# A two-layer encoder with 16 experts: two experts' rows kept on chip, a down product by column halves, the next layer's weights prepared at another place, a norm without GpSimd

## The chip, the cores and the metric

The kernel runs on one core of one Trainium2 chip. TensorE multiplies matrices, VectorE, ScalarE and GpSimd do the element work, and the DMA engines move data; each engine works through its own queue in order and waits at semaphores for the others. SyncE's queue (SP) starts most transfers. The metric is device time in microseconds: the median of several executions. Profiles are of one execution, and times within it count from the start of its span.

## What is computed

Two layers of: a mixer (three kinds of attention behind one input projection), a layer norm, a mixture of 16 experts of which each of 512 tokens takes two, and a layer norm. What matters here is the second half:

```python
h = layer_norm(DEEPNORM_ALPHA * h + mix, ln1_g[l], ln1_b[l])
ffn = grouped_moe(h, router_w, router_bias, exp_w_gate[l], exp_w_up[l], exp_w_down[l])
h = layer_norm(DEEPNORM_ALPHA * h + ffn, ln2_g[l], ln2_b[l])

def grouped_moe(h, ...):                  # h: 512 x 1024, all float32
    ...                                   # gates: two experts per token
    y = jnp.zeros_like(h)
    for e in range(N_EXPERTS):            # 1024 -> 512 -> 1024
        a = jax.nn.silu(h @ w_gate[e]) * (h @ w_up[e])
        y = y + dense_gates[:, e:e + 1] * (a @ w_down[e])
    return y
```

## The kernel before

**Numbers and weights.** A float32 product is made of three matmuls of rounded parts (`mm3`, L399 to L401): high times high, low times high, high times low. So every weight passes through two steps: a high part (`prep_hi`, on ScalarE, L368) and a low part (`prep_lo`, on VectorE, L375, or on GpSimd, L377). Weights stream in as pieces of 512 KB in one fixed list over both layers: `pump` (L323) issues the next load on SP as soon as a buffer is free and the limit `dma_limit` and the cap allow, and `prep` splits pieces up to `look` ahead of the one in use. One piece of each expert product is taken whole in float32 (L1640, L1665) and is not split. Pieces are named "g", "u", "d" for an expert's gate, up and down weights (four of each) and "c0", "c1", ... for the input projection of the next layer.

**An expert.** In `moe`, expert e has a tile of 128 gathered tokens. Its rows come by an indirect load from hD (`start`, L1559), are transposed on TensorE (`trans_x`, L1629) and evacuated in three pieces on ScalarE and VectorE (L1598 to L1600); then come the gate projection, the up projection, the product silu(g) * u (L1735, L1744), its transposes (`trans_a`, L1654) and the down product (`down`, L1665 and `mm3`). The result is scaled by the gate and added to yD in memory by an indirect scatter on GpSimd (L1564). yD starts as a copy of the normed rows, which `w_out` writes beside hD (L1353). The gate projection of expert e+1 is written between the up and the down product of expert e.

**The last expert.** Expert 15 (`LAST`) is not scattered: its scaled rows stay on chip as a high part (L1674, ScalarE) and a low part (L1675, VectorE). After scatter 14, GpSimd loads yD back into h (L1732). `add_rows` multiplies the kept rows by a one-hot matrix for each of four token tiles and two column halves (L1875) and adds them to h with a running sum (L1877, VectorE); the one-hots are transposed beforehand in `last_rows` (L1862, L1863).

**The last norm.** `ln` takes the sum, centres the tile (L719 on ScalarE and L720 on GpSimd for the first three tiles of layer 1, else L722 on VectorE), squares it on ScalarE (L707), raises the variance to the power -0.5 on GpSimd (L709) and makes the final pass on VectorE (L725). In layer 0 the next layer's transposes follow (`make_hT`, L736, evacuated by L738 and L739); in layer 1 each tile goes out by one DMA (L1891).

**What sets the order.** A list scheduler orders the instructions of each engine when the kernel is built, from the order in which the code is written and estimated durations; on the chip each engine keeps that order. `busy(n)` writes n dummy matmuls (L554).

Of the kernel before, what the change touches and what calls it, by code (L numbers as in the profile page):

```python
# [23 lines left out]
S = 512  # L24
# [25 lines left out]
LAST = 15  # L50
# [7 lines left out]
WARM3 = 0  # L58
PRL = (0,)
# [13 lines left out]
LNP = ((), (0, 1, 2))  # L73
# [11 lines left out]
CAPE = 5  # L85
# [174 lines left out]
class Kern:  # L260
# [65 lines left out]
    def prep(self):  # L326
        while self.i_prep < self.i_dma and self.i_prep < self.cur + self.look:
            p = self.pieces[self.i_prep]
            must = self.i_prep == self.cur
            if p.whole:  # L330
                self.i_prep += 1
                p.bufs, p.parts = (p.raw,), ()
                self.prep_low(self.i_prep - 1)
                continue
            if not must and self.used[1] + 2 > self.rcap:
                return
            hi = self.take(self.R)
            lo = self.take(self.R) if hi else None
            if lo is None:
                assert not must, (self.R.free, self.used)  # L340
                if hi:
                    self.give(hi)
                return
            p.bufs = (hi, lo)
            raw, p.hi, p.lo = p.raw.f[:, 0:p.n], hi.r[:, 0:p.n2], lo.r[:, 0:p.n2]
            p.parts = p.split(raw, p.hi, p.lo) if p.split else [(raw, p.hi, p.lo)]
            for (r, hi, lo) in p.parts:
                self.prep_hi(r, hi)
            self.i_prep += 1
            self.prep_low(self.i_prep - 1)  # L350
# [52 lines left out]
    def build_stream(self):  # L403
# [83 lines left out]
        for l in range(DEPTH):  # L487
            for j in range(4):
                P[idx[l, "u%d" % (NE - 1), j]].low = P[idx[l, "d%d" % (NE - 1), j]].low = "v"
                if l:  # L490
                    P[idx[l, "c0", j]].low = "g"
        self.pieces = P
        self.i_dma = self.i_prep = self.i_low = self.n_hi = self.n_lo = 0
        self.dma_limit = len(P)
# [217 lines left out]
    def ln(self, z, sums=None, pool=False, eps=LN_EPS):  # L712
        nc, v = self.nc, self.nc.vector
        self.iw += 1
        w = self.lnbuf[3 + self.iw % 2].f

        def centre(st):
            if pool:
                nc.scalar.activation(w, z, AF.Identity, bias=st[:, 1:2])  # L719
                nc.gpsimd.tensor_tensor(w, w, self.lnrow[0], OP.mult)  # L720
            else:
                v.scalar_tensor_tensor(w, z, st[:, 1:2], self.lnrow[0], op0=OP.add, op1=OP.mult)  # L722

        st = self.ln_stats(z, sums, centre, eps)
        v.scalar_tensor_tensor(z, w, st[:, 4:5], self.lnrow[1], op0=OP.mult, op1=OP.add)  # L725
# [25 lines left out]
    def token_major(self, l, c, evac, pre=None):  # L751
# [5 lines left out]
        for t in range(NT):  # L757
            if pre:
                self.make_hT(t)
                if l == 0 and t == 0:  # L760
                    self.busy(WARM2)
                if l in PRL:
                    if 0 < t < NT - 1:
                        pre(t + 1)
                elif t + 2 < NT:
                    pre(t + 2)
# [527 lines left out]
    def w_out_phase(self, l):  # L1294
# [11 lines left out]
        st, pl = [None] * NT, [None] * NT  # L1306

# [35 lines left out]
        def finish(t, fast):  # L1343
# [8 lines left out]
            for d in (self.hD, self.yD):  # L1352
                nc.sync.dma_start(d[128 * t:128 * (t + 1)], z)  # L1353
# [213 lines left out]
    def moe(self, l):  # L1567
# [88 lines left out]

        def down(e):
            pd = [self.psS.tile([128, 512], F32, name="S") for _ in range(2)]
            for k in range(4):
                i = self.idx[l, "d%d" % e, k]  # L1660
                P = self.get(i)
                for n in range(2):
                    ns = slice(512 * n, 512 * (n + 1))
                    if P.whole:
                        nc.tensor.matmul(pd[n], aW()[:, k], P.raw.f[:, ns], start=k == 0, stop=k == 3)  # L1665
                    else:
                        self.mm3(pd[n], aT(0)[:, k], aT(1)[:, k], P.hi[:, ns], P.lo[:, ns], k == 0, k == 3)
                self.done(i)
            if e >= LAST:
                self.ylast[e] = [self.unit(self.R) for _ in range(2)]  # L1670
                g = gt[e]
                for n in range(2):
                    hi, lo = [x.r[:, 512 * n:512 * n + 512] for x in self.ylast[e]]
                    nc.scalar.activation(hi, pd[n], AF.Copy, scale=g)  # L1674
                    v.scalar_tensor_tensor(lo, pd[n], g, hi.bitcast(F32), op0=OP.mult, op1=OP.subtract)  # L1675
                return
# [4 lines left out]

        i_x = trans_x(0)
        pg[0] = self.psA.tile([128, 512], F32, name="A")
        proj(0, "g", pg[0], 0, 2)
        with self.tc.issue_after(i_x.ins):
            start(1)
        proj(0, "g", pg[0], 2, 4)
# [6 lines left out]
        self.dma_limit = self.idx[l, "d%d" % (NE - 1), 3] + 1  # L1694
        for e in range(NE):
# [34 lines left out]
            if e == NE - 1:  # L1730
# [5 lines left out]
            if e + 1 < NE:  # L1736
                trans_x(e + 1)
            if e + GD < NE:
                start(e + GD)
            if e == NE - 2:  # L1740
                for i in gb:
                    bufs[i].free()
            proj(e, "u", pu[e], 0, 4,
                 lambda: v.tensor_mul(sa[:, 512:1024], sa[:, 0:512], pu[e]))  # L1744
            if e + 1 < NE:
                pg[e + 1] = self.psA.tile([128, 512], F32, name="A")
                proj(e + 1, "g", pg[e + 1], 0, 2, lambda: trans_a(e))
            else:
                trans_a(e)
            if e + GD + 1 < NE:  # L1750
# [3 lines left out]
            down(e)  # L1754
# [126 lines left out]
    def combine(self, l, t):  # L1881
# [3 lines left out]
        self.ln(z, [sm[:, 0:1], sm[:, 1:2]], t in LNP[l], LN_EPS / ALPHA ** 2)  # L1885
# [4 lines left out]
        if l == DEPTH - 1:  # L1890
            self.nc.sync.dma_start(self.out[0, 128 * t:128 * (t + 1)], z)  # L1891
# [150 lines left out]
```

## Time and profile before

| | |
|---|---|
| time, median of 3 runs | 1404.48 us (1400.59 to 1405.84) |
| the profiled execution | 1408.89 us |
| its span | 1406.8 us |
| TensorE busy | 1298.7 us, 92% of the span |
| VectorE busy | 1010.6 us, 72% |
| ScalarE busy | 802.4 us, 57% |
| GpSimd busy | 285.9 us, 20% |
| moved by DMA | 291.10 MB, mean 207 GB/s |

The profiled execution took 2.1 us more than its span. Busy matmul time is modelled, so a busy TensorE is not one at its peak; the granted clock tells at which of its two levels (1.2 or 2.4 GHz) a stretch ran, as a share of the full one. Layer 0's experts lie between about 355 and 682 us, layer 1's between about 1026 and 1378 us.

### The profile page before, as it was taken

What the parts mean: (1) busy time and instruction counts of PE and PEld (TensorE: products, weight loads), DVE (VectorE), ACT (ScalarE), POOL (GpSimd) and SP (SyncE); (2) the same over time, 40 slices, a digit from 0 to 9 for tenths busy, and PEclk for the clock granted to TensorE, in tenths of its full rate; (3) what the DMA queues carried; (4) which work ended last, traced back from release to release, by engine and by line L of the source; (5) the groups of instructions that cost most, each with busy time, mean ns of one, the idle gap of its engine ahead of it and who ended that gap; (6) DMA issues with size and microseconds to landing.
All of it is one profiled execution on the core that took longest, in us unless ns stands there. A gap on an engine that the chain in (4) does not pass through costs nothing. (4 is left out here: it accounts for less than half of the span.)

```text
span 1406.8 us, 18646 instructions
## 1 busy us (share of the span) xinstructions
PE 1298.7 (92%) x5986; PEld 959.7 (68%) x5994; DVE 1010.6 (72%) x2268; ACT 802.4 (57%) x1428; POOL 285.9 (20%) x217
## 2 busy tenths in 40 slices
PE   7999999989999999899699999998989999969993
PEld 5786766668677776676478666676867777656761
DVE  5768977766778777777445798868668877757765
ACT  5467855651566665566336776556146666545662
POOL 1012213332111111111300222234212111102113
PEclk8999999999999999999799999999999999989997
DMA  8411313356699998999610133315759999879983
GB/s 259 125 31 31 109 61 91 113 186 240 200 310 319 321 351 268 341 384 314 222 42 16 36 93 102 120 52 189 270 168 301 312 319 366 248 252 320 382 298 120
DMA packets 114138, 291.10 MB, mean 207 GB/s; under 512 B 19719, under 2 KB 42503, under 8 KB 114033
## 3 DMA queue, kind: packets, MB, share of 16 engines
q1 hardware_dynamic: 97824, 255.35, 51.7%
q0 software_dynamic: 11424, 32.43, 9.6%
q10 hardware_dynamic: 4784, 2.05, 0.6%
q8 instruction: 50, 0.82, 0.2%
q14 instruction: 56, 0.45, 0.1%
HBM read 268.13 MB, written 28.05 MB: 211 GB/s over the span
## 5 line engine op out<-in xcount | busy, mean ns | idle before, releaser
L368 ACT ACTIVATE slot<-arena 128x1024 fp32r<-128x1024 f32 (+3 forms) x145 | 125.7, 885 | 118.8 <-PE A L401 28.0
L368 ACT ACTIVATE slot<-slot 128x1024 fp32r<-128x1024 f32 x105 | 110.8, 1059 | 88.3 <-PE A L401 41.1
L375 DVE TENSOR_TENSOR slot<-slot,slot 128x1024 fp32r<-128x1024 f32 x99 | 121.0, 1224 | 54.7 <-ACT slot L368 51.4
L401 PE MATMUL S<-slot,rounded 128*128 128x512 f32 x368 | 151.2, 411 | 0.0
L401 PE MATMUL A<-slot,rounded 128*128 128x512 f32 x364 | 144.7, 398 | 0.0
L399 PE MATMUL S<-slot,rounded 128*128 128x512 f32 x312 | 137.5, 442 | 7.1 <-ACT rounded L738 4.6
L375 DVE TENSOR_TENSOR slot<-arena,slot 128x1024 fp32r<-128x1024 f32 (+2 forms) x95 | 105.6, 1113 | 43.8 <-ACT slot L368 41.7
L1564 POOL DMA_INDIRECT yD<-arena,ix x30 | 50.1, 1670 | 416.8 <-ACT rounded L1599 207.0
L400 PE MATMUL S<-slot,rounded 128*128 128x512 f32 x312 | 127.7, 409 | 3.3 <-DVE rounded L739 2.0
L399 PE MATMUL A<-slot,rounded 128*128 128x512 f32 x276 | 121.4, 440 | 0.6 <-ACT rounded L738 0.6
L377 POOL TENSOR_TENSOR slot<-arena,slot 128x1024 fp32r<-128x1024 f32 (+4 forms) x50 | 80.1, 1617 | 174.7 <-ACT slot L368 153.5
L400 PE MATMUL A<-slot,rounded 128*128 128x512 f32 x276 | 109.9, 398 | 0.8 <-DVE rounded L739 0.8
L1955 ACT ACTIVATE arena<-arena,ast 128x256 f32<-128x256 f32 (+3 forms) x160 | 88.9, 557 | 32.7 <-DVE ast L1944 23.5
L368 ACT ACTIVATE rounded<-slot 128x1024 fp32r<-128x1024 f32 x74 | 78.5, 1061 | 44.2 <-PE A L400 27.7
L399 PE MATMUL S<-rounded,slot 128*128 128x512 f32 (+1 forms) x224 | 90.5, 406 | 0.0
L400 PE MATMUL S<-rounded,slot 128*128 128x512 f32 (+1 forms) x224 | 90.0, 402 | 0.0
L401 PE MATMUL S<-rounded,slot 128*128 128x512 f32 (+1 forms) x224 | 89.3, 399 | 0.0
L401 PEld LDWEIGHTS S<-slot,rounded 128*128 128x128 f32 x368 | 72.0, 196 | 16.8 <-DVE slot L1809 0.8
L399 PE MATMUL A<-rounded 128*128 128x512 f32 x172 | 81.5, 474 | 0.1
L1986 ACT ACTIVATE slot<-T 128x128 fp32r<-128x128 f32 (+3 forms) x128 | 53.4, 431 | 48.2 <-PE T L1981 47.5
L401 PEld LDWEIGHTS A<-slot,rounded 128*128 128x128 f32 x364 | 68.7, 189 | 15.9
L1640 PE MATMUL A<-slot,arena 128*128 128x512 f32 x168 | 79.3, 593 | 0.0
(365 smaller groups left out, 3062.1 us busy)
## 6 DMA issues: line engine op xcount, KB each, us to landing
slot<-in_exp_w_down_dram SPq DMA_DIRECT2D x80, 512.0 KB, 7.2
slot<-in_exp_w_up_dram SPq DMA_DIRECT2D x73, 512.0 KB, 6.9
slot<-in_exp_w_gate_dram SPq DMA_DIRECT2D x72, 512.0 KB, 6.9
arena<-in_exp_w_gate_dram SPq DMA_DIRECT2D x60, 512.0 KB, 6.5
arena<-in_exp_w_up_dram SPq DMA_DIRECT2D x59, 512.0 KB, 7.1
arena<-in_exp_w_down_dram SPq DMA_DIRECT2D x52, 512.0 KB, 6.9
arena<-in_w_in_dram SPq DMA_DIRECT2D x17, 512.0 KB, 5.5
slot<-in_w_in_dram SPq DMA_DIRECT2D x9, 512.0 KB, 6.1
```

Of the source, the lines that this page charges most:

```text
L368: self.nc.scalar.activation(hi, r, AF.Copy)
L375: self.nc.vector.tensor_sub(lo, r, hi.bitcast(F32))
L377: self.nc.gpsimd.tensor_tensor(lo, r, hi.bitcast(F32), OP.subtract)
L399: t.matmul(ps, xh, wh, start=start, stop=False)
L400: t.matmul(ps, xl, wh, start=False, stop=False)
L401: t.matmul(ps, xh, wl, start=False, stop=stop)
L1564: self.nc.gpsimd.indirect_dma_start(out=self.yD[:, :], out_offset=bass.IndirectOffsetOnAxis(ap=ix[:, 0:1], axis=0), in_=y, in_offset=None, ...
L1640: nc.tensor.matmul(ps, xW(e)[:, kk], P.raw.f[:, 512 * k:512 * k + 512], start=kk == 0, stop=kk == 7)
L1955: nc.scalar.activation(p, p, AF.Exp, bias=self.st[:, m:m + 1], scale=-1.0, accum_out=self.st[:, 2 + m:3 + m])
L1986: nc.scalar.activation(self.part(0), self.ps, AF.Copy)
```

## The change

- `LAST` is 14: the rows of experts 14 and 15 both stay on chip, and `add_rows` has four matmuls instead of two for each tile and half. The reload of h is written at expert 14, behind scatter 13. The last buffer of scattered rows is freed one expert earlier.
- `down_last`: expert 15's down product takes all four pieces for the left column half, keeps it, and then does the right half.
- The high and low parts of the next layer's pieces may be written right behind `trans_a(15)` (`prep_limit`), up to eight raw buffers may be used for them (`CAPE`), and the low parts of c0 are no longer on GpSimd. 18 dummy matmuls are written ahead of layer 1's first `make_hT`.
- The last norm does not use ScalarE and GpSimd for centring; its final pass and its output write are made by halves, the second half's write on ScalarE's queue.
- The writes of yD are issued behind all hD writes, in `moe` after the first gate matmuls. The transposes of expert 1 are written behind expert 0's up projection.

```diff
-LAST = 15
+LAST = 14
+WARM4 = 18
-LNP = ((), (0, 1, 2))
+LNP = ((), ())
-CAPE = 5
+CAPE = 8
...
-        while self.i_prep < self.i_dma and self.i_prep < self.cur + self.look:
+        while self.i_prep < min(self.i_dma, self.prep_limit, self.cur + self.look):
...
-                if l:
-                    P[idx[l, "c0", j]].low = "g"
...
-        v.scalar_tensor_tensor(z, w, st[:, 4:5], self.lnrow[1], op0=OP.mult, op1=OP.add)
+        if out is None:
+            v.scalar_tensor_tensor(z, w, st[:, 4:5], self.lnrow[1], op0=OP.mult, op1=OP.add)
+            return
+        for n in range(2):
+            ns = slice(512 * n, 512 * n + 512)
+            v.scalar_tensor_tensor(z[:, ns], w[:, ns], st[:, 4:5], self.lnrow[1][:, ns], op0=OP.mult, op1=OP.add)
+            (nc.scalar if n else nc.sync).dma_start(out[:, ns], z[:, ns])
...
+                if l and t == 0:
+                    self.busy(WARM4)
...
-            for d in (self.hD, self.yD):
-                nc.sync.dma_start(d[128 * t:128 * (t + 1)], z)
+            self.i_hd.append(nc.sync.dma_start(self.hD[128 * t:128 * (t + 1)], z))
...
+        def keep_rows(e, pd, n):
+            if n == 0:
+                self.ylast[e] = [self.unit(self.R) for _ in range(2)]
+            hi, lo = [x.r[:, 512 * n:512 * n + 512] for x in self.ylast[e]]
+            nc.scalar.activation(hi, pd, AF.Copy, scale=gt[e])
+            v.scalar_tensor_tensor(lo, pd, gt[e], hi.bitcast(F32), op0=OP.mult, op1=OP.subtract)
...
+        def down_last(e):
+            ids = [self.idx[l, "d%d" % e, k] for k in range(4)]
+            P = [self.get(i) for i in ids]
+            for n in range(2):
+                pd = self.psS.tile([128, 512], F32, name="S")
+                for k in range(4):
+                    down_mm(e, P[k], pd, k, n)
+                keep_rows(e, pd, n)
+            for i in ids:
+                self.done(i)
...
+        with ExitStack() as after:
+            for i in self.i_hd:
+                after.enter_context(self.tc.issue_after(i.ins))
+            for t in range(NT):
+                nc.sync.dma_start(self.yD[128 * t:128 * (t + 1)], self.h[:, t])
...
-            if e == NE - 1:
+            if e == LAST:
...
-            if e + 1 < NE:
+            if 0 < e < NE - 1:
...
+            if e == 0:
+                trans_x(1)
...
+                self.prep_limit = len(self.pieces)
+                self.budget(14, 2)
...
-            down(e)
+            (down if e + 1 < NE else down_last)(e)
...
-        self.ln(z, [sm[:, 0:1], sm[:, 1:2]], t in LNP[l], LN_EPS / ALPHA ** 2)
+        self.ln(z, [sm[:, 0:1], sm[:, 1:2]], t in LNP[l], LN_EPS / ALPHA ** 2,
+                None if l < DEPTH - 1 else self.out[0, 128 * t:128 * (t + 1)])
...
-        if l == DEPTH - 1:
-            self.nc.sync.dma_start(self.out[0, 128 * t:128 * (t + 1)], z)
```

Lines move by 1 (L399 becomes L400) to some 35 (L1875 becomes L1910). On TensorE at the MoE start of layer 0, before: the rows from the whole-precision part of expert 0's up projection (L1640) on.

```order
L1640 MATMUL A<-arena 128x512 x2
L1629 MATMUL T<-cst,arena 128x128 x8
L399 MATMUL A<-rounded 128x512
L400 MATMUL A<-rounded 128x512
L401 MATMUL A<-rounded 128x512
```

And now, the end of the same up projection and the start of expert 1's gate projection (L1647).

```order
L401 MATMUL A<-slot_3294,rounded 128x512
L402 MATMUL A<-slot_3295,rounded 128x512
L1636 MATMUL T<-cst,arena 128x128 x8
L1647 MATMUL A<-slot_2534,arena 128x512 x2
L400 MATMUL A<-rounded 128x512
```

The eight transposes of expert 1's rows stood ahead of the split part of expert 0's up projection and now stand behind its last matmul.

On ScalarE at the end of layer 0, before: three splits of expert 15's down weights, the evacuation of its activations (L1598, L1599), four splits of c0 between the two kept halves (L1674), and the squares of the norm.

```order
L368 ACTIVATE slot_6251<-arena 128x1024
L368 ACTIVATE slot_6261<-arena 128x1024
L368 ACTIVATE slot_6272<-arena 128x1024
L1598 ACTIVATE arena<-T 128x128
L1599 ACTIVATE rounded<-T 128x384
L368 ACTIVATE slot_6284<-arena 128x1024
L368 ACTIVATE slot_6310<-arena 128x1024
L368 ACTIVATE slot_6322<-arena 128x1024
L1674 ACTIVATE rounded<-S,gt 128x512
L368 ACTIVATE slot_6334<-arena 128x1024
L1674 ACTIVATE rounded<-S,gt 128x512
L707 ACTIVATE arena,bst<-h,bst 128x1024 x2
```

And now: the seven splits (slots 6333, 6321, 6315 and 6327 are c0's), the evacuation (L1605, L1606), both kept halves (L1669) and one split of c1.

```order
L369 ACTIVATE slot_6271<-arena 128x1024
L369 ACTIVATE slot_6333<-slot_6274 128x1024
L369 ACTIVATE slot_6282<-arena 128x1024
L369 ACTIVATE slot_6294<-arena 128x1024
L369 ACTIVATE slot_6321<-slot_6265 128x1024
L369 ACTIVATE slot_6315<-arena 128x1024
L369 ACTIVATE slot_6327<-slot_6267 128x1024
L1605 ACTIVATE arena<-T 128x128
L1606 ACTIVATE rounded<-T 128x384
L1669 ACTIVATE slot_6350<-S,gt 128x512 x2
L369 ACTIVATE slot_6369<-arena 128x1024
L706 ACTIVATE arena,bst<-h,bst 128x1024 x2
```

All four splits of c0 moved from behind the evacuation of expert 15's activations to ahead of it.

On GpSimd at the end of layer 1, before and then now:

```order
L569 DMA arena<-in_ln_b_dram 128x1024
L568 DMA arena<-in_ln_g_dram 128x1024
L1564 DMA yD<-arena,ix 640x1024
L1732 DMA h<-yD 128x1024 x4
L720 TENSOR_TENSOR arena<-arena 128x1024
L709 TENSOR_TENSOR bst<-bst,mhalf 128x1
L720 TENSOR_TENSOR arena<-arena 128x1024
```

```order
L1571 DMA yD<-arena,ix 640x1024
L1763 DMA h<-yD 128x1024 x4
L568 DMA arena<-in_ln_b_dram 128x1024
L567 DMA arena<-in_ln_g_dram 128x1024
L708 TENSOR_TENSOR bst<-bst,mhalf 128x1 x4
```

The scatter of expert 14 is gone, the reload of h moved ahead of the norm's rows and behind the scatter of expert 13, and the centring left this queue.

## Rows read from the trace of the kernel before

**Rows 1.** Stretches: us, busy time (instructions) by engine, granted clock, DMA share, GB/s.

```profile
1050.00:1190.00 140.00, 140.00 (x602) 101.17 (x601) 109.68 (x170) 89.59 (x118) 23.18 (x14) 1.00 0.96 320
...
675.00:680.00 5.00, 2.52 (x11) 1.69 (x9) 0.00 (x0) 2.00 (x2) 1.65 (x1) 1.00 1.04 409
```

**Rows 2.** TensorE's waits in the whole span: total us, times, longest.

```profile
PE S L1875 <- ACT rounded L1674: 7.5, 3, 5.1
PE T L1629 <- DMA arena<-hD,ix: 7.1, 2, 4.8
```

**Rows 3.** ScalarE's longest waits from 1050 to 1190.

```profile
ACT slot L368 <- PE A L401: 15.3, 18, 2.3
```

**Rows 4.** Timeline at both MoE starts: start, us, instruction, idle before and releaser.

```profile
362.22 1.58 PE L1629 MATMUL T<-cst,arena 128*128 128x128 f32 x8 [2.27 <-DMA arena<-hD,ix]
...
369.13 1.88 PE L1640 MATMUL A<-slot,arena 128*128 128x512 f32 x4
...
1028.94 1.96 PE L1640 MATMUL A<-arena 128*128 128x512 f32 x4
...
1035.74 1.94 PE L1629 MATMUL T<-cst,arena 128*128 128x128 f32 x8 [4.84 <-DMA arena<-hD,ix]
...
1042.38 1.88 PE L1640 MATMUL A<-arena 128*128 128x512 f32 x4
```

**Rows 5.** Timeline at layer 0's end; scatters' landing; low parts (page: busy, mean ns).

```profile
643.90 1.81 POOL L1564 DMA_INDIRECT yD<-arena,ix  x1 [14.52 <-ACT rounded L1599]
...
665.13 7.89 SPq L323 DMA_DIRECT2D arena<-in_w_in_dram  x4
...
669.66 3.55 PE L1665 MATMUL S<-slot,arena 128*128 128x512 f32 x4 [0.37 <-ACT arena L1598]
...
677.21 2.00 ACT L368 ACTIVATE slot<-arena 128x1024 fp32r<-128x1024 f32 x2 [7.22 <-DMA arena<-in_w_in_dram]
...
681.95 0.67 ACT L1674 ACTIVATE rounded<-S,gt 128x512 fp32r<-128x512 f32 x1
...
684.72 1.06 ACT L368 ACTIVATE slot<-arena 128x1024 fp32r<-128x1024 f32 x1 [2.10 <-DMA arena<-in_w_in_dram]
...
693.09 1.28 DVE L725 SCALAR_TENSOR_TENSOR h<-arena,bst 128x1024 f32<-128x1024 f32 x1
...
694.52 1.94 PE L736 MATMUL T<-cst,h 128*128 128x128 f32 x8 [3.71 <-DVE h L725]
...
DMA to landing us min/median/max: 6.2/9.1/12.5
...
L375 DVE TENSOR_TENSOR slot<-slot,slot 128x1024 fp32r<-128x1024 f32 x99 | 121.0, 1224 | 54.7 <-ACT slot L368 51.4
```

**Rows 6.** Timeline of layer 1's tail; landing of the output writes.

```profile
1379.71 0.69 DVE L1877 SCALAR_TENSOR_TENSOR h<-S,h 128x512 f32<-128x512 f32 x1
...
1381.65 0.15 DVE L702 TENSOR_TENSOR bst<-csum 128x1 f32<-128x1 f32 x1
...
1383.79 2.35 POOL L720 TENSOR_TENSOR arena<-arena 128x1024 f32<-128x1024 f32 x1 [9.79 <-ACT arena L719]
...
1384.35 1.81 DVE L702 TENSOR_TENSOR bst<-csum 128x1 f32<-128x1 f32 x1
...
1387.53 3.37 DVE L725 SCALAR_TENSOR_TENSOR h<-arena,bst 128x1024 f32<-128x1024 f32 x1 [0.56 <-POOL bst L709]
...
1393.00 3.25 DVE L722 SCALAR_TENSOR_TENSOR arena<-h,bst,arena 128x1024 f32<-128x1024 f32 x1
...
1398.99 1.28 DVE L725 SCALAR_TENSOR_TENSOR h<-arena,bst 128x1024 f32<-128x1024 f32 x1 [0.66 <-POOL bst L709]
...
DMA to landing us min/median/max: 2.6/2.6/2.6
```

**Rows 7.** All instructions of two lines: ns min/median/max, first and last start.

```profile
L1862 PE MATMUL T<-cst,arena x8: 271/272/273, 660.4 to 1363.1; 128*128 128x128 f32 x8
...
L554 PE MATMUL A<-mchunk,b_zero x46: 323/326/524, 1.4 to 13.5; 128*1 128x384 bf16 x46
```

More of the change, by code (lines that the diff above doesn't have):

```diff
@@ L489, in build_stream @@
                 P[idx[l, "u%d" % (NE - 1), j]].low = P[idx[l, "d%d" % (NE - 1), j]].low = "v"
[L490 to L491 removed]
         self.pieces = P
         self.i_dma = self.i_prep = self.i_low = self.n_hi = self.n_lo = 0
[L494 removed]
+        self.dma_limit = self.prep_limit = len(P)
         self.pat_hi, self.pat_lo = "a", "v"
@@ L710, in ln_stats, with ln @@
         return st
-    def ln(self, z, sums=None, pool=False, eps=LN_EPS):
+    def ln(self, z, sums=None, pool=False, eps=LN_EPS, out=None):
         nc, v = self.nc, self.nc.vector
@@ L1306, in w_out_phase @@
         st, pl = [None] * NT, [None] * NT
+        self.i_hd = []
         self.G = [self.psA.tile([128, 512], F32, name="A") for _ in range(2)]
@@ L1655, in trans_a, with down_mm @@
             parts(ps, aW(), aT(0), aT(1))
+        def keep_rows(e, pd, n):
[4 more added lines that the diff above has]
+            v.scalar_tensor_tensor(lo, pd, gt[e], hi.bitcast(F32), op0=OP.mult, op1=OP.subtract)
+        def down_mm(e, P, pd, k, n):
+            ns = slice(512 * n, 512 * (n + 1))
+            if P.whole:
+                nc.tensor.matmul(pd, aW()[:, k], P.raw.f[:, ns], start=k == 0, stop=k == 3)
+            else:
+                self.mm3(pd, aT(0)[:, k], aT(1)[:, k], P.hi[:, ns], P.lo[:, ns], k == 0, k == 3)
         def down(e):
@@ L1662, in down @@
                 for n in range(2):
[L1663 to L1667, printed above, removed]
+                    down_mm(e, P, pd[n], k, n)
                 self.done(i)
             if e >= LAST:
-                self.ylast[e] = [self.unit(self.R) for _ in range(2)]
-                g = gt[e]
                 for n in range(2):
-                    hi, lo = [x.r[:, 512 * n:512 * n + 512] for x in self.ylast[e]]
-                    nc.scalar.activation(hi, pd[n], AF.Copy, scale=g)
-                    v.scalar_tensor_tensor(lo, pd[n], g, hi.bitcast(F32), op0=OP.mult, op1=OP.subtract)
+                    keep_rows(e, pd[n], n)
                 return
@@ L1693, in moe @@
         self.ht, self.hts, self.ylast = {}, [], {}
-        self.dma_limit = self.idx[l, "d%d" % (NE - 1), 3] + 1
+        self.dma_limit = self.prep_limit = self.idx[l, "d%d" % (NE - 1), 3] + 1
         for e in range(NE):
```

## The prediction

> **What bounds the kernel now.** I read TensorE by stages first, then what it waited for, then what the engine that prepares its weights waited for, and last the order in time at the places where TensorE stood still. Inside the experts it has no hole: 140.00 of 140.00 us busy in a stretch of layer 1, with 602 matmuls, so 0.233 us each, at full clock [rows 1]. ScalarE's splits wait there for TensorE to give buffers back [rows 3], so weights come in time, although the DMA engines' share in the same stretch is 0.96 [rows 1]. An edit inside the experts can only add matmuls or not; what can be gained lies in the holes. TensorE's waits name the ones that this change touches [rows 2]: 7.1 us in two places for a gather (the MoE starts), and 7.5 us for the last expert's kept rows, nearly all at the end of layer 0. At that end it also waits 3.71 us for the norm [rows 5]. After the last matmul comes a tail of VectorE, ScalarE and GpSimd [rows 6].
>
> **MoE start (transposes of expert 1 behind expert 0's up projection).** TensorE stops before the eight transposes until the gather has landed, and 18 matmuls of the up projection, which need nothing of it, stand behind them [rows 4]. In layer 1 the whole-precision part of that projection starts at 1028.94 and takes 1.96 us, the transposes begin at 1035.74, and expert 1's gate projection at 1042.38. Turned round, the 18 matmuls run from 1030.9 for 18 x 0.233 = 4.2 us to 1035.1; the gather lands at 1035.7; the transposes take about 1.0 us instead of 1.94 if the clock stays up; their evacuation, with one split of 1.06 us ahead of it on ScalarE, takes some 1.1 us: the gate projection at 1037.8, a gain of 4.6 us. In layer 0 the stop of 2.27 us ended at 362.22 and the gate projection started at 369.13; the same working (gather at 362.2, matmuls to 364.2, transposes, evacuation) gives 366.4, a gain of 2.7. Against it, the yD writes are now issued behind all hD writes, the fourth close to the gather: 512 KB at the 320 GB/s of [rows 1] are 1.6 us, of which the gather feels 0 to 1.3, and in layer 1 that would show in full. Bounds: 2 to 3.5 and 3.5 to 5.8.
>
> **End of layer 0.** Three things followed each other [rows 5]. The next layer's first weights (four loads of 512 KB) were issued from 665.13 on, over 7.89 us. ScalarE's queue has their splits ahead of the last expert's kept rows, and it sat waiting for them: the first at 677.21 after 7.22 us of idle, the last at 684.72 after 2.10. The down product, four whole-precision matmuls in 3.55 us from 669.66 and 18 of 0.233, was done at about 677.4, but the first half of the kept rows came at 681.95. The norm's first tile was ready at 694.37 (693.09 + 1.28), and the transposes for the next projection began at 694.52. Now these loads and the reload of h stand behind the scatter of expert 13, issued at 643.90. Scatters took 6.2 to 12.5 us to land; with the median of 9.1 the first two pieces are issued near 654, the other two near 661, as buffers come free. All four splits now stand ahead of the evacuation of the last expert's activations on ScalarE, and one low part ahead of their product on VectorE, both queues in order: behind a split that waits are queued the evacuation, and behind that TensorE's whole down product. If the last piece takes 7 to 9 us it is there at 668 to 670, the evacuation is done at 671.3 and the down product starts at 671.8, 2.1 later than before. It runs at full clock, since dummies stand where TensorE idled: 18 x 0.233 and four whole ones in 1.9 (as the four at 1042.38 [rows 4]) are 6.1 us, to 677.9. The second half's kept rows take 0.67 on ScalarE (the length of the row at 681.95) and about as long on VectorE, to 679.4. VectorE then needs four sums of 0.69, one low part of 1.22, a centring and a final pass of 1.28 each, and 0.9 for small ones and the power: 7.4 us. The first tile is ready at 686.8 and the transposes start 7.6 us earlier; I take 7.2, since the norm's rows and other tiles share VectorE. Bounds: 2, if the last piece takes 12 us, as the first one did before (665.13 to 677.21), and the evacuation waits until 674; 10.5, if no split waits. The four low parts cost VectorE 4 x 1.22 = 4.9 us that GpSimd had; VectorE was busy 0.00 of the 5 us from 675 [rows 1], which is where they hide, and without that cover they would be 4.9 us of path.
>
> **Tail.** GpSimd's centring beside VectorE makes three VectorE instructions long [rows 6]: a 128x1 sum takes 1.81 us instead of 0.15 and ends when GpSimd's 2.35 us end; a final pass takes 3.37 instead of 1.28, a centring 3.25. That is 1.66 + 2.09 + 1.97 = 5.7 us, all on the chain, since VectorE idles there only in four waits for the power of 0.56 to 0.66. Without GpSimd they come back, and VectorE does three centrings more, 3 x 1.28 = 3.8. Eight final passes of half width (0.69, as a 128x512 sum) instead of four of 1.28 cost 0.4. Two of the four waits are now covered by work that stands behind them: 0.9 less. That is 2.4 us. The last output write is half as large, at 320 GB/s 0.8 us less at most; I take 0.4. Gain 2.8, bounds 1.5 to 4.5. The down product by halves gives nothing here: the second half is still evacuated behind the last matmul, and VectorE's first sum stands behind that.
> The four old output writes landed 2.6 us after issue, each alone [rows 6]. The Trainium skill (DMA: Bandwidth & Descriptors, Issuing engines are not separate DMA queues) says that transfers started by different engines end up on the same 16 DMA engines and interleave, which speaks against the second queue: by it the 0.4 would be due to the first half's earlier issue alone, and if both halves came at once the sum would be poorer by 0.4. No run here shows two output queues at once.
>
> **What the change adds.** Expert 14's one-hot transposes and their copies stand in the full expert stretch of both layers: four transposes of 0.27 [rows 7] and what they displace, 0.6 to 1.5 us a layer; I take 0.8, so 1.6. Of 16 more adding matmuls a layer, those of three tiles lie in holes; four stand inside the next projection, 4 x 0.233 = 0.9. One weight load is issued ahead of the overflow tile's, 0 to 1.6 us; I take 0.8. The 18 dummies lie in holes before the transposes, before the down product and between sums; at the low clock one costs 0.33 [rows 7], and those that don't fit add up to 3 us, which the lower bound of the transition holds. Scaling expert 14's rows twice instead of once takes ScalarE and VectorE 0.7 us each, off the path while TensorE is full; if that cover were gone it would be 0.7 a layer. The scatter that goes was on GpSimd, which nobody waits for inside the experts.
>
> **Sum.** -2.7 - 4.6 - 7.2 - 2.8 + 1.6 + 0.9 + 0.8 = -14.0 us. The profiled execution took 1408.89 us (its span of 1406.8 and 2.1 around it), 4.4 above the median of the runs; it would become 1394.9. Taken off the median, 1404.48 - 14.0 = 1390.5.
>
> **Rivals.**
> 1. The weights' stream is the bound. For it: a DMA share of 0.96 in the experts. What TensorE gains at the two MoE starts it then waits for later, in front of weights: -7.2 - 2.8 + 3.3 = -6.7, so 1397.8. Against it: ScalarE waited for TensorE, not for weights [rows 3]. Chance 0.14.
> 2. The next layer's pieces land 12 us after issue, as before; the transition gives 2 to 3: 1395.2. Chance 0.12.
> 3. Slower than before, by the same wait made longer. Each microsecond by which the last piece lands after 669 is one of the down product, since the evacuation stands behind its split. At 683, 22 us after issue, the whole gain is gone; at 25 us it is 1407.5, at 29 us 1411.5. For it: the last expert's weights, the reload of h and the norm's rows all want the DMA engines between 654 and 670. Against it: 12 us was what a piece took before, with the engines fully busy (share 1.04 from 675 on [rows 1]). Chance 0.04.
> 4. The change doesn't do what it says: the dummies don't hold the clock and run in TensorE's path, and the first tile of the norm comes no earlier. -2.7 - 4.6 - 2.8 + 3.3 = -6.8, and up to 3 for dummies: 1397.7 to 1400.7. Chance 0.06.
> 5. More than that: no split waits and every gain is at its upper bound, every cost at its lower: 3.5 + 5.8 + 10.5 + 4.5 - 2.2 = 22: 1382.4. Chance 0.06.
> The forecast, 1386 to 1395, has the rest, 0.58.
>
> **How the numbers follow.** About 0.5% (7 us) is what a measurement of this kernel can tell from no change; faster by more means under 1397.5. That holds the forecast 0.58, half of the first rival 0.07, the second 0.12 and the fifth 0.06: 0.83. Slower by more: 0.03 of the third and 0.02 for what I don't see, 0.05. The rest, 0.12, is the same. The range of 8 in 10 takes in the first two rivals and stops short of the fifth: 1383 to 1399.
>
> **What would show it.** TensorE's wait for the gather before expert 1's transposes should be under 1 us in both layers. From the last expert's first whole-precision down matmul to the first transposes of layer 1's input there should be some 15 us (before 669.66 to 694.52, 24.9). ScalarE should wait under 3 us for the next layer's pieces. No VectorE instruction of the tail should be longer than 1.4 us, and from its first sum to the end of the last pass there should be about 18.2 us (1379.71 to 1400.27, 20.6). A wait of TensorE inside the experts for weights that are not split, or one of ScalarE of 5 us or more ahead of the last evacuation, would make the sum wrong.

## The result, and the profile after

The changed kernel takes 1391.34 us (median; 1390.85 to 1393.26), the kernel before 1404.52 beside it: a ratio of 0.9894, 95% interval 0.9873 to 0.9916. In a second comparison on another chip the ratio was 0.9894 again (0.9861 to 0.9926), with runs of the changed kernel spread from 1385.6 to 1398.6. The forecast was 1390.5. The profiled execution took 1390.85 us, its span 1389.1; the one of before had been 4.4 us above its median, so the two profiles differ by 18.0 us and the medians by 13.2.

MoE starts, which answer to [rows 4]. Timeline of TensorE: start, duration, instruction, idle before and what ended it.

```profile
356.61 1.10 PE L1647 MATMUL A<-arena 128*128 128x512 f32 x2
...
363.65 1.05 PE L1636 MATMUL T<-cst,arena 128*128 128x128 f32 x8
...
365.23 1.98 PE L1647 MATMUL A<-slot,arena 128*128 128x512 f32 x4 [0.53 <-ACT arena L1605]
...
1021.06 1.10 PE L1647 MATMUL A<-arena 128*128 128x512 f32 x2
...
1027.81 1.13 PE L1636 MATMUL T<-cst,arena 128*128 128x128 f32 x8
...
1029.33 1.98 PE L1647 MATMUL A<-arena 128*128 128x512 f32 x4 [0.39 <-ACT arena L1605]
```

The transposes no longer wait for the gather, and they take 1.05 and 1.13 us (granted clock 1.00) instead of 1.58 and 1.94 (0.67 and 0.50). From the up projection's first whole matmul to expert 1's gate projection there are 8.62 and 8.27 us instead of 11.14 and 13.44. In layer 0 of the kernel before, that first matmul is this one:

```profile
357.99 1.96 PE L1640 MATMUL A<-arena 128*128 128x512 f32 x4
```

The end of layer 0, which answers to [rows 5]: timeline of the changed kernel.

```profile
649.99 7.73 SPq L324 DMA_DIRECT2D slot<-in_w_in_dram  x3
...
662.73 0.40 PE L402 MATMUL A<-slot,rounded 128*128 128x512 f32 x1
663.06 1.46 PE L553 MATMUL A<-mchunk,b_zero 128*1 128x384 bf16 x8
666.56 1.06 ACT L369 ACTIVATE slot<-slot 128x1024 fp32r<-128x1024 f32 x1 [6.53 <-DMA slot<-in_w_in_dram]
667.52 1.99 ACT L369 ACTIVATE slot<-arena 128x1024 fp32r<-128x1024 f32 x2
...
669.92 0.68 DVE L1775 TENSOR_TENSOR arena<-arena,A 128x512 f32<-128x512 f32 x1
...
670.66 1.13 PE L1661 MATMUL T<-cst,arena 128*128 128x128 f32 x4 [6.14 <-DVE arena L1775]
...
671.72 2.40 PE L553 MATMUL A<-mchunk,b_zero 128*1 128x384 bf16 x7
672.26 0.25 ACT L1605 ACTIVATE arena<-T 128x128 f32<-128x128 f32 x1
...
674.05 2.08 PE L1675 MATMUL S<-slot,arena 128*128 128x512 f32 x2
...
690.00 1.94 PE L741 MATMUL T<-cst,h 128*128 128x128 f32 x8 [2.42 <-DVE bst L703]
```

Here little was gained. The kept rows no longer wait, but TensorE stands for 6.14 us one step earlier, before the transposes of expert 15's activations: ScalarE waits 6.53 us for one of the next layer's pieces, and two splits of expert 15's own down weights stand behind it; VectorE's product L1775 stands behind the low parts of that piece and of the first of these, and the transposes wait for the product. On ScalarE three more splits of c0 stand ahead of the evacuation at 672.26, 5.7 us after the end of the wait. The last up matmul ends at 663.1, and layer 1's transposes start 26.9 us later; it was 27.6 before, where the last up matmul is this one:

```profile
666.54 0.40 PE L401 MATMUL A<-slot,rounded 128*128 128x512 f32 x1
```

(On ScalarE before, three of the four splits of c0 stood ahead of the first kept half and one between the halves; not all four stood between them.)

The tail, which answers to [rows 6]: VectorE in the changed kernel, the first sum, two passes of half width, the longest instructions, the last pass.

```profile
1365.13 0.68 DVE L1912 SCALAR_TENSOR_TENSOR h<-S,h 128x512 f32<-128x512 f32 x1
...
1369.33 0.15 DVE L701 TENSOR_TENSOR bst<-csum 128x1 f32<-128x1 f32 x1
...
1376.12 1.28 DVE L721 SCALAR_TENSOR_TENSOR arena<-h,bst,arena 128x1024 f32<-128x1024 f32 x1
...
1378.13 1.42 DVE L729 SCALAR_TENSOR_TENSOR h<-arena,bst 128x512 f32<-128x512 f32 x2 [0.41 <-POOL bst L708]
...
1381.47 1.42 DVE L729 SCALAR_TENSOR_TENSOR h<-arena,bst 128x512 f32<-128x512 f32 x2 [0.66 <-POOL bst L708]
```

No VectorE instruction is longer than 1.28 us (the 1.42 are two), and from the first sum to the last pass's end there are 17.8 us instead of 20.6.

**Stage by stage.** The next table is worked out from each kernel's timeline, in us between marks: MoE start (first gate matmul to expert 1's gate projection), experts (from there to the last up matmul's end), end of layer 0 (from there to layer 1's first transposes), input projection (from there to the transposes of L847, which follow it), mixer (to the first gate matmul), sums (last up matmul's end to the first sum), tail (to the end of the last pass), output (to the span's end).

| stage | before | before again | changed | changed again | splits behind (e2) | e11 |
|---|---|---|---|---|---|---|
| start of the span to layer 0's MoE | 351.7 | 353.6 | 350.3 | 352.4 | 348.0 | 351.8 |
| MoE start, layer 0 | 17.5 | 17.5 | 14.9 | 14.9 | 14.9 | 14.9 |
| experts, layer 0 | 297.8 | 298.3 | 297.9 | 300.7 | 299.7 | 300.2 |
| end of layer 0 | 27.6 | 27.9 | 26.9 | 21.6 | 18.2 | 17.4 |
| input projection | 38.5 | 38.3 | 36.2 | 37.0 | 35.6 | 35.6 |
| mixer, layer 1 | 289.6 | 289.5 | 288.6 | 289.6 | 289.4 | 289.2 |
| MoE start, layer 1 | 19.8 | 19.3 | 14.6 | 15.0 | 14.6 | 14.7 |
| experts, layer 1 | 326.9 | 325.7 | 325.5 | 329.4 | 325.9 | 327.5 |
| sums | 10.5 | 10.5 | 10.3 | 11.9 | 9.5 | 9.5 |
| tail | 20.6 | 20.5 | 17.8 | 17.8 | 17.8 | 17.8 |
| output | 6.5 | 6.5 | 6.2 | 6.2 | 6.2 | 6.2 |

What repeats within 0.5 us is the MoE starts, the tail and the output. The first 350 us, the mixer and the experts differ between executions of one kernel by as much as between kernels, so 1.4 + 1.0 + 1.4 = 3.8 us of the 17.7 by which the two spans differ lie in stretches where no run shows the edit to act.

### The profile page after: what moved, and what is told of

Read it like the earlier page. It is cut to its first block, busy times and chain, and to the rows that moved or that the text cites. A ratio compares the mean times of both kernels' runs of the same rounds, so it can differ in the third digit from the quotient of the medians.

```text
span 1389.1 us, 18769 instructions
## 1 busy us (share of the span) xinstructions
PE 1303.3 (94%) x6052; PEld 961.6 (69%) x6052; DVE 1016.0 (73%) x2289; ACT 800.3 (58%) x1429; POOL 267.3 (19%) x208
## 5 line engine op out<-in xcount | busy, mean ns | idle before, releaser
L376 DVE TENSOR_TENSOR slot<-slot,slot 128x1024 fp32r<-128x1024 f32 x105 | 128.3, 1225 | 64.7 <-ACT slot L369 61.9
L369 ACT ACTIVATE slot<-slot 128x1024 fp32r<-128x1024 f32 x111 | 117.1, 1058 | 100.4 <-PE A L402 36.7
L402 PE MATMUL A<-slot,rounded 128*128 128x512 f32 x372 | 147.7, 397 | 0.0
L400 PE MATMUL S<-slot,rounded 128*128 128x512 f32 x316 | 138.9, 442 | 6.4 <-ACT rounded L743 4.0
L376 DVE TENSOR_TENSOR slot<-arena,slot 128x1024 fp32r<-128x1024 f32 (+2 forms) x101 | 112.8, 1120 | 42.8 <-ACT slot L369 40.5
L400 PE MATMUL A<-slot,rounded 128*128 128x512 f32 x288 | 125.4, 435 | 0.3 <-ACT rounded L743 0.3
L1571 POOL DMA_INDIRECT yD<-arena,ix x28 | 46.9, 1674 | 408.1 <-ACT rounded L1606 197.5
L401 PE MATMUL A<-slot,rounded 128*128 128x512 f32 x288 | 114.1, 396 | 0.4 <-DVE rounded L744 0.4
L378 POOL TENSOR_TENSOR slot<-arena,slot 128x1024 fp32r<-128x1024 f32 (+4 forms) x46 | 70.7, 1550 | 170.2 <-ACT slot L369 148.6
L369 ACT ACTIVATE rounded<-slot 128x1024 fp32r<-128x1024 f32 x70 | 74.3, 1061 | 44.6 <-PE A L401 25.5
L400 PE MATMUL S<-rounded,slot 128*128 128x512 f32 (+1 forms) x224 | 90.5, 406 | 0.0
L402 PEld LDWEIGHTS S<-slot,rounded 128*128 128x128 f32 x368 | 70.9, 193 | 17.7 <-DVE slot L1844 2.0
L1647 PE MATMUL A<-slot,arena 128*128 128x512 f32 x168 | 79.4, 594 | 0.5 <-ACT arena L1605 0.5
L400 PEld LDWEIGHTS S<-slot,rounded 128*128 128x128 f32 x316 | 61.1, 194 | 25.4 <-ACT rounded L743 5.0
```

Of the source, the lines that this page charges most:

```text
L369: self.nc.scalar.activation(hi, r, AF.Copy)
L376: self.nc.vector.tensor_sub(lo, r, hi.bitcast(F32))
L378: self.nc.gpsimd.tensor_tensor(lo, r, hi.bitcast(F32), OP.subtract)
L400: t.matmul(ps, xh, wh, start=start, stop=False)
L401: t.matmul(ps, xl, wh, start=False, stop=False)
L402: t.matmul(ps, xh, wl, start=False, stop=stop)
```

## The experiments

Each profile is of one execution; times of e1, e3 and e5 to e9 are single runs.

**e1: the kernel before, again.**

> The kernel before once more, to see where its profiled execution of 1408.9 us, 4.4 above the median, lost time. If the surplus lies in one stage, that stage's distance differs from the first profile by about 4 us. If the stages repeat within 0.5 us each, the surplus is spread, and the stage by stage differences between the two kernels can be taken as they are.

1409.6 us. Its stages repeat the first profile's within 1.9 us (table above), most of them within 0.5, and no stage holds 4 us: the surplus of profiled executions of this kernel over its median stays unexplained.

**e2 and e11: the next layer's splits held behind the evacuation.**

```diff
-                trans_a(e)
+                i_low = trans_a(e)
+                held = ExitStack()
+                held.enter_context(self.tc.issue_after(self.i_evac.ins))   # ScalarE, L1606
+                held.enter_context(self.tc.issue_after(i_low.ins))         # VectorE, L1607
                 self.prep_limit = len(self.pieces)
                 self.budget(14, 2)
+                self.prep()
 ...
             (down if e + 1 < NE else down_last)(e)
+            if e + 1 == NE:
+                held.close()
```

> The changed kernel, with the four splits of the next layer's pieces held behind the evacuation of the last expert's activations on ScalarE and VectorE; nothing else differs. Theory A: in the changed kernel these splits stand ahead of the evacuation and wait 6.5 us for a piece, and that wait is path. Then TensorE's stop before the last transposed activations falls from 6.1 us to under 2, the down product starts about 8 us earlier, layer 1's first transposes come 6 to 8 us earlier, and the time is 1383 to 1386. Rival: the splits then queue among the kept rows and the norm's sums, 4 x 1.05 us on ScalarE and 4 x 1.22 on VectorE, and take most of it back: transposes 0 to 3 us earlier, 1388 to 1391.

1384.44 us, ratio to before 0.9858 (0.9832 to 0.9884). Timeline at the same place:

```profile
662.65 0.69 DVE L1775 TENSOR_TENSOR arena<-arena,A 128x512 f32<-128x512 f32 x1 [0.48 <-PE A L402]
663.45 0.75 PE L1661 MATMUL T<-cst,arena 128*128 128x128 f32 x4
664.24 0.28 ACT L1605 ACTIVATE arena<-T 128x128 f32<-128x128 f32 x1 [1.92 <-PE T L1661]
664.71 1.12 PE L1675 MATMUL S<-slot,arena 128*128 128x512 f32 x2
...
667.21 1.06 ACT L369 ACTIVATE slot<-slot 128x1024 fp32r<-128x1024 f32 x1 [1.37 <-DMA slot<-in_w_in_dram]
...
670.45 1.24 ACT L1669 ACTIVATE slot<-S,gt 128x512 fp32r<-128x512 f32 x2
...
680.86 1.13 PE L741 MATMUL T<-cst,h 128*128 128x128 f32 x8 [1.67 <-DVE bst L703]
```

The product waits 0.48 us, for its own last matmul; the down product starts 2.1 us after that matmul's end instead of 10.9; and the splits wait for their pieces while TensorE multiplies. Transposes come 8.6 us sooner after the last up matmul (18.2 for 26.9; 3.3 sooner than in e10's profile), and the input projection is not longer for it (35.6). Theory A held, and the rival didn't: the splits in front of the kept rows cost little.

It isn't quite so that nothing else differs. In both layers the low part of the last split piece of expert 15's down weights moved from ahead of the product L1775 to behind the evacuation too. In layer 1, where no next layer follows, TensorE's wait before the last transposes is halved by that; the changed kernel, then e2:

```profile
1356.42 0.74 PE L1661 MATMUL T<-cst,arena 128*128 128x128 f32 x4 [1.61 <-DVE arena L1775]
```

```profile
1347.20 0.75 PE L1661 MATMUL T<-cst,arena 128*128 128x128 f32 x4 [0.78 <-DVE arena L1775]
```

The sums take 9.5 us in e2 and e11 instead of 10.3 and 11.9, so 0.8 us or more of the gain of this order comes from layer 1.

> The splits behind the evacuation once more, beside the changed kernel: 0.984 to 0.987 of the kernel before, 6 to 7 us less than the changed kernel, with no run of either between the two groups if the order of the splits is the cause.

Beside the changed kernel on one chip: 1383.06 us (1380.4 to 1386.8), ratio 0.9834 (0.9813 to 0.9855), against 1394.03 (1385.6 to 1398.6) and 0.9894 for the changed kernel (e10). The ranges overlap by 1.2 us, against the expectation; the intervals of the ratios don't. The gain is larger than expected, 11.0 us by the medians.

> The changed kernel again, beside the next two on the same chip: 0.988 to 0.991 of the kernel before.

In e10's profile (1398.3 us) the pieces landed sooner after their issue, and the end of layer 0 took 21.6 us instead of 26.9. What it lost against the first profile is spread: 2.1 us ahead of the first MoE, 2.8 and 3.9 in the experts, 2.2 in the input projection, the mixer and the MoE start of layer 1 together, and 1.6 in the sums, where the last down product ran partly at the low clock: granted 0.84 from 1362 to 1373, against 1.00 in the same work of the first profile.

```profile
1362.00:1373.00 11.00, 10.40 (x35) 7.30 (x36) 2.59 (x5) 2.03 (x4) 0.00 (x0) 0.84 0.00 1
```

**e3: why the piece is late.** The reload of h is left out in layer 0.

```diff
-                for t in range(NT):
+                for t in range(NT if l else 0):
                     nc.gpsimd.dma_start(self.h[:, t], self.yD[128 * t:128 * (t + 1)])
```

> The changed kernel without layer 0's reload of h from yD (2 MB on GpSimd's queue), so h lacks the other experts' sums there. Theory A, with its reason: the DMA engines are full (about 400 GB/s) from 640 to 666 us, and the reload is 2 MB of that, so without it the next layer's pieces land about 5 us earlier, ScalarE's wait of 6.5 us falls to 1 to 2, and layer 1's first transposes start 4 to 5 us earlier. Rival: the pieces land late because of buffers and SP's own queue; the wait stays within 1 us of 6.5.

Routing in layer 1 changes with h, so this run tells only of layer 0. Stretches of the changed kernel and then of e3 (busy times, granted clock, DMA share, GB/s), and ScalarE's wait for the pieces in each:

```profile
640.00:667.00 27.00, 24.52 (x101) 17.09 (x99) 14.94 (x19) 12.83 (x17) 4.46 (x7) 1.00 1.00 366
...
ACT slot L369 <- DMA slot<-in_w_in_dram: 6.5, 1, 6.5
```

```profile
640.00:667.00 27.00, 26.98 (x114) 18.96 (x113) 20.48 (x25) 18.60 (x25) 2.97 (x3) 1.00 0.88 289
...
ACT slot L369 <- DMA slot<-in_w_in_dram: 0.6, 1, 0.6
```

With the reload the DMA engines are full (share 1.00) and the piece issued at 649.99 is waited for until 666.56; without it they are not, the piece issued at 653.91 is there when ScalarE comes to it at 663.55, and a later one is waited for 0.6 us. The transposes of the activations then start 1.3 us after the last up matmul's end, not 7.5. In the other profiles with reload and splits as in the changed kernel (e5 to e7, e9, e10) ScalarE waits 3.2 to 6.5 us, so e3's 0.6 lies outside what executions differ by. So the piece is late because the reload that the change put beside it takes the same engines.

**e4: without the new place of the splits.** `prep_limit` and `budget(14, 2)` are taken out.

> The changed kernel without the new place of the next layer's splits (no own limit for splits, no larger budget behind the last transposed activations). One split of c0 then stands ahead of the evacuation, two between the two kept halves, one behind. Theory A: this undo makes the kernel faster, 1384 to 1388, since the wait ahead of the evacuation shrinks to 0 to 3 us and the pieces have landed by the time of the kept rows. Rival: the new place is what the change gained at this point, and the time rises to 1393 to 1396.

1391.29 us, ratio 0.9904 (0.9883 to 0.9924): the same as the changed kernel, so neither theory's number. The stages tell why. The end of layer 0 falls to 19.5 us, as theory A said, but the input projection rises to 39.4 (35.6 to 37.2 where the splits are early and the dummies stand). The sums take 11.9, but so they do in e10. The first 6 us of that projection in e4 and then in e2:

```profile
681.00:687.00 6.00, 5.65 (x21) 4.27 (x22) 5.50 (x9) 3.34 (x6) 1.74 (x2) 0.72 0.00 0
```

```profile
680.90:686.90 6.00, 5.26 (x26) 4.31 (x27) 5.74 (x11) 3.46 (x6) 0.55 (x1) 1.00 0.01 3
```

In e4 it begins partly at the low clock (0.72), after TensorE had waited 3.4 us for the norm (1.7 in e2), and seven shorter waits for evacuated tiles follow. Early splits are worth 2 to 4 us there; their place ahead of the evacuation costs 2 to 7 (21.6 and 26.9 for 19.5). e2 keeps the one and drops the other.

**e5 and e6: the MoE start.** e5 puts `trans_x(1)` back in front of the up projection, e6 puts each yD write back behind its hD write.

> The changed kernel with the transposes of expert 1 ahead of expert 0's up projection again. Theory: the order alone made the gain at the two MoE starts, so from the first whole matmul of the up projection to the first of expert 1's gate projection it takes 11 us or more again in layer 0 (8.6 in the changed kernel) and 13.4 in layer 1 (8.3), with TensorE's waits for the gather of about 2.3 and 4.8 us back, or up to 1.3 more each where the fourth write of yD shares the engines; the time rises by 7 to 9 us. Rival: the earlier gather or the moved writes made part of it; then less than 5 us come back.

1403.56 us. The two stretches of 8.62 and 8.27 us are 14.36 and 13.84 again:

```profile
359.77 1.96 PE L1647 MATMUL A<-arena 128*128 128x512 f32 x4
366.56 1.95 PE L1636 MATMUL T<-cst,arena 128*128 128x128 f32 x8 [4.83 <-DMA arena<-hD,ix]
...
1026.90 1.96 PE L1647 MATMUL A<-arena 128*128 128x512 f32 x4
1033.95 1.94 PE L1636 MATMUL T<-cst,arena 128*128 128x128 f32 x8 [5.08 <-DMA arena<-hD,ix]
```

The two MoE starts take 20.7 and 20.2 us, 5.8 and 5.6 more than in the changed kernel, which is more than the change had gained there. So the order alone makes the gain. In layer 0 the wait is 4.83 us, not the 2.27 of [rows 4]: the gather took 7.1 us from issue to landing, 4.5 before, with the fourth write of yD issued 2.2 us ahead of it, and only the new order hides that.

> The changed kernel with each write of yD behind its write of hD again. Theory: the writes between the hD writes held up the end of the mixer's output stage; in the changed kernel the stretch from the stage's first transposes to the first gate matmul was 1.0 us shorter in layer 0 and 0.2 in layer 1, and these come back, while the gather is there in time in both: 1 to 1.5 us slower in all. Rival: the moved writes cost the gather time in the changed kernel, so undoing it gains: the waits for the gather go from 0.2 us to none and the time doesn't rise.

1394.84 us, a single run within the changed kernel's spread. The stretches at the MoE starts are 8.62 and 8.26 us, as in the changed kernel. The output stage of layer 0's mixer took 50.2 us (48.6 in the changed kernel), but also 50.2 in e7 and e8, which have the moved writes. So no effect of these writes on the time is seen either way. On the gather of layer 0 there is one: with the writes back it took 4.6 us, with the moved writes 6.2 (e10) to 7.2 (e7).

**e7: GpSimd back in the last norm.** `LNP = ((), (0, 1, 2))`.

> The changed kernel with the last norm's centring of three tiles on ScalarE and GpSimd again. Theory: VectorE's long instructions come back (a 128x1 sum of 1.5 us or more, passes of 2 to 3 us), and from the first sum to the end of the last pass it takes 20 to 21 us instead of 17.8; the time rises by 2.5 to 3. Rival: the halved passes (0.69 us each) fit between GpSimd's instructions better than whole ones, and only 0 to 1.5 us come back.

```profile
1373.14 1.13 DVE L701 TENSOR_TENSOR bst<-csum 128x1 f32<-128x1 f32 x1
...
1374.83 3.50 DVE L729 SCALAR_TENSOR_TENSOR h<-arena,bst 128x512 f32<-128x512 f32 x2
...
1380.38 2.30 DVE L701 TENSOR_TENSOR bst<-csum 128x1 f32<-128x1 f32 x1
```

1396.44 us, a single run. The long instructions are back, and the tail takes 20.2 us instead of 17.8: 2.5 us, as worked out.

**e8 and e12: one expert kept.** `LAST = 15` in e8; in e12 it is 14 in layer 0 and 15 in layer 1, on e2's order.

> The changed kernel with only expert 15's rows kept (the reload of h behind scatter 14, two adding matmuls for each tile and half). Theory A: without the reload's 2 MB in front of them three of the next layer's pieces land before 665, so the last transposed activations start 4 to 6 us earlier than in the changed kernel (7.7 us after the last up matmul there); but the fourth piece waits for scatter 14, lands near 680, and its split stands ahead of the kept rows on ScalarE: layer 1's first transposes within 2 us of the changed kernel's, 690. So keeping expert 14 pays at the kept rows and takes back at the activations; the time 1390 to 1394. Rival, the prediction's reason: the earlier loads are the gain; without them the transposes are 5 us or more later, 1396 or more.

1389.58 us, a single run within the changed kernel's spread. The end of layer 0 takes 24.1 us, the sums 9.4 and the tail 18.3. With the changed splits, then, no gain from keeping expert 14 is seen. The reload comes later, but so do the loads: the first three of c0 are issued from 657.03 on, not from about 650, ScalarE waits 5.6 us for two of them, and TensorE's stop of 3.95 us lies within the 2.5 to 6.2 of the profiles with splits and reload as in the changed kernel (e5 to e7, e9, e10). Of theory A's details, three pieces by 665 and transposes of the activations 4 to 6 us earlier did not come, and the fourth piece came at 673.6, not near 680.

> As the one before, but in layer 1, where no next layer's weights follow, only expert 15's rows are kept. Theory: keeping expert 14 costs layer 1 1.5 us (its one-hots in the full expert stretch and two more matmuls before the first sum, as the kernel with one kept expert in both layers showed), and nothing there needs the early reload; 1 to 2 us less than the one before, 0.983 to 0.986. Rival: the reload behind scatter 14 comes late for the first sums and takes it back: no difference, or slower.

1388.05 us, ratio 0.9855 (0.9833 to 0.9877); e11 had 0.9834 (0.9813 to 0.9855). The ratio is the expected one, but it is not 1 to 2 us less than the one before: the medians lie 5.0 us the other way. The sums are 0.9 shorter (8.6 for 9.5) and the tail 0.5 longer (18.3 for 17.8), so the two stages give 0.4 in all. The intervals overlap; whether it pays is open. No run keeps only expert 15 in layer 0 with e2's order, so what keeping expert 14 is worth there is open too.

**e9: no dummies.** `WARM4 = 0`.

> The changed kernel without its 18 dummy matmuls at the end of layer 0. Theory (the prediction's): they keep the granted clock up, so without them the four whole matmuls of the down product take 3.5 us instead of 2.1 + 1.0, the down product ends 1 to 2 us later, and so do the transposes; the time rises by 1 to 2 us. Rival: TensorE waits long enough there for other reasons that the clock falls anyway or the loss hides: within 0.5 us at layer 1's first transposes.

```profile
670.92 1.13 PE L1661 MATMUL T<-cst,arena 128*128 128x128 f32 x4 [6.21 <-DVE arena L1775]
672.82 2.08 PE L1675 MATMUL S<-slot,arena 128*128 128x512 f32 x2 [0.77 <-ACT arena L1605]
```

1395.11 us, a single run within e10's range, so the expected 1 to 2 us can't be told from it. The two whole matmuls take 2.08 us with and without dummies, at a granted clock of 0.50: behind that stop the dummies did not keep it up. The down product starts 1.9 us after the transposes here; in the changed kernel's profile it is 3.4, because the seven dummies between them took 2.40 us at the low clock. The end of layer 0 is 1.6 us shorter (25.3 for 26.9), the input projection 2.2 longer (38.4 for 36.2). From the first gate matmul to the end of the input projection it is 376.1 us against 375.9 (e10: 374.3). In these profiles, what the dummies give later they take here, where TensorE has stood 6 us before them. In e10, where it had stood 2.55 us, the same seven took 1.30:

```profile
672.00 0.75 PE L1661 MATMUL T<-cst,arena 128*128 128x128 f32 x4 [2.55 <-DVE arena L1775]
672.68 1.30 PE L553 MATMUL A<-mchunk,b_zero 128*1 128x384 bf16 x7
```

Stretches of these seven, in the changed kernel and in e10 (busy times, granted clock, DMA share, GB/s):

```profile
671.70:674.10 2.40, 2.40 (x9) 0.77 (x8) 2.36 (x4) 1.19 (x3) 0.00 (x0) 0.50 1.12 350
```

```profile
672.70:674.00 1.30, 1.28 (x8) 0.48 (x7) 0.82 (x2) 1.30 (x2) 0.00 (x0) 1.00 1.16 305
```

## Why the prediction was right, and where it was not

The total was right and one large term was not. The prediction's own sign that its sum was wrong, a wait of ScalarE of 5 us or more ahead of the last evacuation, came (6.53 us), and the sum came out all the same.

- **MoE starts:** forecast 2.7 and 4.6, measured 2.5 and 5.2 (14.9 for 17.5, 14.6 for 19.8). Shown by e5: the order alone. The gather's delay by the fourth write, which the sum bounded by 1.3 us, was 2.6 in e5's layer 0 (4.83 for 2.27); in the changed kernel it is hidden.
- **End of layer 0:** forecast 7.2, less 0.9 in the next projection; measured 0.7 there and 2.3 in the projection, 3.0 instead of 6.3. The step that failed is the landing: "7 to 9 us" after issue. The issues came as forecast (near 654 and 661 in the times of the kernel before; the last up matmul ends 3.8 us earlier in the changed kernel, which makes them 650 and 657), but the piece issued at 649.99 was waited for until 666.56. The sum also goes by the last piece alone, as if the splits ahead of it were done by then; behind the piece that was waited for, five more splits, 4.7 us, stood ahead of the evacuation. The second rival had the mechanism, with 12 us; and of what the prediction lists "for it" in the third rival, e3 shows the reload. Two steps behind it failed too: "it runs at full clock" (2.08 us for two whole matmuls, 1.02 at full clock), and the dummies that "lie in holes": seven of them were about 1.5 us of path (3.4 for 1.9 in e9). Their price at the low clock, 0.33, was read from rows at a granted clock of 1.00, where 45 of them took 8.89 us; that it fits (2.40 us for seven) is luck. How much is lost differs by execution: the end of layer 0 takes 26.9, 21.6, 21.2, 25.8 and 26.9 us in the five profiles in which nothing of it was edited (the changed kernel, e10, e5, e6, e7).
- **The transition without the waiting splits** was sized rightly: where no split stands in the way (e2, e11), the end of layer 0 takes 17.4 to 18.2 us, 9 to 10 less than before, near the upper bound of 10.5. How much of this the earlier loads give, the kept rows of expert 14 or the down product by halves is not shown: no run takes one of these out of e2, and e8, with the splits in the way, saw no loss.
- **Tail:** forecast 2.4 and 0.4 for the output, measured 2.8 and 0.3, and e7 gives 2.5 back. The terms (5.7 returned, 3.8 added) are borne out by the rows: no VectorE instruction is long, and four centrings of 1.28 us stand where one stood. The passes and the output by halves have no run of their own. On the output the Trainium skill (DMA: Bandwidth & Descriptors, Issuing engines are not separate DMA queues) says that queues of several engines share the 16 DMA engines. The trace of the changed kernel agrees as far as it goes: in the tail the two queues (packets, MB, share of 16 engines) moved 1.05 MB each, never faster than 384 GB/s in a slice of 0.5 us, where one queue had gone over 400 before. The 0.3 us fit a smaller last write; no run shows that it is the cause.

```profile
q1 hardware_dynamic: 576, 1.05, 13.4%
q10 hardware_dynamic: 576, 1.05, 13.2%
```

- **Costs inside the experts:** 1.6 + 0.8 us were added; the profiles show no difference above the 1 to 4 us by which these stages vary (297.8 to 297.9, 326.9 to 325.5). For layer 1, the stages of e11 and e12 put the price of keeping expert 14 at 0.9 in the sums, less 0.5 in the tail, but their medians differ by 5.0 us the other way.
- **Why the sum came out:** in the profiles, 2.5 + 3.0 + 5.2 + 3.1 + 0.1 (sums), 14.0 us before rounding, lie where the edit acts, against a forecast of 14.0: the missing 3.3 us at the end of layer 0 were balanced by costs of 2.4 that didn't show and by 0.9 more at the MoE starts, the sums and the tail together. The medians differ by 13.2. It was right in part by errors that cancel.

## What to carry to other kernels

A split or copy that waits for a transfer blocks all that stands behind it on an in-order queue, so work for the next stage belongs behind the last instruction that the current stage needs from that engine, not merely where its data were planned to be ready: here that is 7 to 11 us of 1391 by the medians of e2 and e11. When loads are moved earlier, count the bytes that then meet in one stretch; a landing time read where the DMA engines had room doesn't hold where they are full. And where a stall is removed, look one step ahead on the same queues for the stall that takes its place.

## What the runs showed of the hardware

- A 512 KB transfer was there up to 16.6 us after its issue with the DMA engines' share at 1.00 and 366 GB/s over 27 us; with the 2 MB of the reload taken away the share was 0.88 at 289 GB/s, and ScalarE's wait for such pieces fell from 6.5 to 0.6 us.
- Seven small dummy matmuls took 1.30 us (granted clock 1.00) when TensorE had idled for 2.55 us before the preceding transposes, and 2.40 us (0.50) when it had idled for 6.14: behind the longer stop the dummies ran at the low level themselves.
- The 512 KB gather of layer 0 took 4.5 and 4.6 us from issue to landing (the kernel before, e6), and 6.2 to 7.2 us with a 512 KB write issued 2.2 us ahead of it (e10, e5, e7). In layer 1 it took 7.1 us in the kernel before without that write, for a reason that no run shows.
- Executions of one kernel differ in stretches that no edit touches: the first gate matmul came between 348.0 and 355.5 us in the profiles of this study, with the same work ahead of it but for four writes.
